# Some transfers move from SP to ACT's queue, and keys come in fewer, larger loads

## The chip, the cores and the metric

The kernel runs on one core of one Trainium2 chip. The metric is the time of one execution on the device in microseconds; the median of the runs shown is 1557.02 us. TensorE (PE), VectorE (DVE), ScalarE (ACT), GpSimd (POOL) and SyncE (SP) each work through an instruction list of their own in order. A transfer is issued by one engine's queue, and that engine goes on to its next instruction once the issue is done.

## The reference

One layer of an encoder runs on a prompt of 2048 tokens and a sample of 512, each of 1024 features, in float32:

```python
h = _rms_norm(x, norm_w)
proj = h @ w_in
# split in 15 parts: a_u, a_v, a_z, b_q, ..., c_q, c_k, c_v, c_z, d_x, d_z
y_a = _sgu_mixer(a_u, a_v, sgu_w, sgu_b) * silu(a_z)
y_b = _deltanet_mixer(b_q, b_k, b_v, ...) * silu(b_z)      # recurrence over chunks, both directions
y_c = _attention_mixer(c_q, c_k, c_v, ...) * silu(c_z)     # 4 heads of 64, 2 key heads, all tokens
y_d = _pool_mixer(d_x, pool_w, pool_scale) * silu(d_z)
return x + concat([y_a, y_b, y_c, y_d]) @ w_out
```

The attention's softmax runs over all tokens of a sequence: 2048 keys for each query of the prompt, 512 for the sample's.

## The kernel before

Tokens are taken in five blocks of 512, four of the prompt and one of the sample. Numbers that need more than half precision are split in two float16 parts whose products are summed, so most matrix products are three matmuls. Between stages the data pass through scratch tensors in DRAM.

`phase1` projects, convolves and normalises the delta-rule inputs. `phase2` runs in three passes over the blocks with other columns of `w_in`: rotary queries and keys (stored by `store_qk` to `QS` and `KS`), gates (`gz`, `zz`, `accz` on PE, from tiles `xs` that `load_xs` reads), pooling. Meanwhile `recurrence` steps through the chunks (tiles `kx`, `kv`, `at`, `tt` in; `up` on PE; `r`, `v`, `s` on ACT; `S` on DVE; `o` to `OD`). Each mixer's part of the concatenated row is written by `store_mix`: ACT writes `mixs`, DVE its second half, SP stores it to `MIX[b][f]`, f from 0 to 7.

`phase3` is attention and output projection. `load_kv` loads the keys of both key heads: `ka` holds both float16 parts of the keys on 128 rows, `kb` the first part again on 64 rows with a row of ones. `load_q` loads one head's queries of a block (`qa` twice the first part, `qb` the second). For a head, `row_max` computes scores `mp` on PE, DVE takes their maxima `mm`, and PE turns these (`mr`) for a row that ACT writes into `qb`. `attn` then goes through the keys in steps of 128: two matmuls give `sp`, ACT computes `e = exp(sp)` and its float16 copy `p`, DVE (every fourth time POOL) the second part of `p`, and PE adds twelve small matmuls to `O`. The next head's `row_max` is interleaved.

`outproj` loads a block's eight `MIX` parts (`mx`) and for each of four token tiles the input `xr`, computes `op` with 48 matmuls, adds on DVE to `y`, and stores `y`. Its matmuls are units that `pump` hands out one after each attention step at low priority, so that they fill PE.

The order on each engine isn't written by hand. A planner (`TileContext(..., schedule_with_timeline_sim=True)`) simulates the program with its own estimates of durations and takes, by priority, what is ready; each engine then runs its list in that order. Transfers of SP and ACT signal on eight completion semaphores that the planner gives out in turn over both queues, and each waits for the one before it on its semaphore.

Of the kernel before, what the change touches and what calls it, by code (L numbers as in the profile page):

```python
# [8 lines left out]
F16 = mybir.dt.float16  # L9
# [35 lines left out]
class Trunk:  # L45
# [94 lines left out]
    def consts(self, ctx):  # L140
        tc, nc, I = self.tc, self.nc, self.I
        self.cp = cp = self.pool(ctx, "const")
        self.nw = cp.tile([128, 8], F32, name="nw")
        self.ident = cp.tile([128, 128], F32, name="ident")
        self.ps = ctx.enter_context(tc.tile_pool(name="psum", bufs=1, space=PSUM))
        self.dram = ctx.enter_context(tc.tile_pool(name="dram", bufs=1, space=DRAM))
        NB, NT = self.NB, self.NT
        d = self.dram
        self.XS = [d.tile([128, 2, 8, 512], F16, name=f"xs{b}") for b in range(NB)]
        self.KX = [d.tile([4, 3, 64, 4, 2, 128], F16, name=f"kx{b}") for b in range(NB)]  # L150
        self.KV = [d.tile([4, 128, 512], F32, name=f"kv{b}") for b in range(NB)]
        self.MIX = [[d.tile([128, 2, 512], F16, name=f"mix{b}_{f}") for f in range(8)] for b in range(NB)]
        self.DG = [d.tile([128, 1024], F32, name=f"dg{b}") for b in range(NB)]
        self.XL = [d.tile([128, 1024], F32, name=f"xl{b}") for b in range(NB)]
        self.OD = [d.tile([128, 4, 256], F32, name=f"od{b}") for b in range(NB)]
        self.AT = [[d.tile([128, 2, 512], F16, name=f"at{t}_{i}") for i in range(2)] for t in range(NT)]
        self.SZ = [[d.tile([128, 512], F32, name=f"sz{b}_{f}") for f in range(4)] for b in range(NB)]
        self.QS = [d.tile([2, 4, 64, 512], F16, name=f"qs{b}") for b in range(NB)]
        self.KS = [d.tile([2, 2, 64, 512], F16, name=f"ks{b}") for b in range(NB)]
        self.TT = [[d.tile([128, 2, 512], F16, name=f"tt{t}_{i}") for i in range(2)] for t in range(NT)]  # L160
        self.DIF = [[d.tile([128, 512], F32, name=f"dif{b}_{f}") for f in range(2)] for b in range(NB)]
        self.MXD = [[d.tile([128, 512], F32, name=f"mxd{b}_{f}") for f in range(2)] for b in range(NB)]
        self.VT = [d.tile([128, 4, 260], F16, name=f"vt{b}") for b in range(NB)]
        self.LCJ = cp.tile([128, NT, 8], F32, name="lcj")
        self.C16 = cp.tile([128, NT, 3, 8], F16, name="c16")
        self.EG = [cp.tile([128, NT, 4], F32, name=f"eg{i}") for i in range(2)]
        self.NEG = [cp.tile([128, NT, 4], F32, name=f"neg{i}") for i in range(2)]
        self.KDS = [cp.tile([128, NT, 4], F32, name=f"kds{i}") for i in range(2)]
        self.EGT = cp.tile([128, NT, 8], F32, name="egt")
        self.RQK = cp.tile([128, NT, 8], F32, name="rqk")  # L170
# [393 lines left out]
    def phase2(self, names, ep, shared, stop=None):  # L564


        tc, nc, I = self.tc, self.nc, self.I
        V, A, G, PE = nc.vector, nc.scalar, nc.gpsimd, nc.tensor
        NB, W = self.NB, self.W2
# [111 lines left out]

        def store_qk(dst, s):

            if s.shape[2] == 2:
                for half in range(2):
                    for hl in range(2):
                        nc.sync.dma_start(dst[hl, :, half * 32:half * 32 + 32, :], s[:, hl, half, :])
            else:
                for half in range(2):
                    for hl in range(2):  # L690
                        nc.sync.dma_start(dst[hl, :, half * 32:half * 32 + 32, :], s[half * 64:half * 64 + 64, hl, 0, :])

        def rope_q(a, c, cs):

# [24 lines left out]
        def finish_k(b, kt, rt):  # L719
            s = ep.tile([128, 2, 2, 512], F16, tag="qk16", name="k16", bufs=1)[:, :, 0:1]  # L720
            with urgent():
                rb = norm_spread(rt, 2)
                V.tensor_tensor(kt, kt, rb, op=ALU.mult)
            A.activation(s[:, 0, 0], kt, AF.Copy)
            G.tensor_tensor(s[:, 1, 0], kt, s[:, 0, 0], op=ALU.subtract)
            store_qk(self.KS[b], s)

        def later(ins):

# [59 lines left out]
        for b in range(NB if stop is None else stop):  # L789
# [12 lines left out]
            if "QA" in names or "C" in names:  # L802
                t0 = b * 512 - (0 if b * 512 < self.NP else self.NP)
# [20 lines left out]
            if "C" in names:  # L824
                kt, ks = [ep.tile([128, 512], F32, tag=f"k{i}", name="k", bufs=1) for i in range(2)]
# [22 lines left out]
    def phase3(self, kp, ap, wp, ep, e5, rest, post):  # L848


        tc, nc, I = self.tc, self.nc, self.I
        V, A, G, PE, NB = nc.vector, nc.scalar, nc.gpsimd, nc.tensor, self.NB
        if True:
            wo = []
            for k in range(8):
                t = wp.tile([128, 2, 1024], F16, name=f"wo{k}")
# [9 lines left out]
            def load_q(b, h):  # L866
                qa = ap.tile([128, 512], F16, tag="qa", name="qa")
                qb = ap.tile([65, 512], F16, tag="qb", name="qb")
                for i in range(2):
                    nc.sync.dma_start(qa[i * 64:i * 64 + 64, :], self.QS[b][0, h])  # L870
                nc.sync.dma_start(qb[0:64, :], self.QS[b][1, h])
                return qa, qb

            def row_max(seq, b, h):
# [66 lines left out]
            def outproj(b):  # L941
                mix = []
                for f in range(8):
                    p, tag, n = (pool5(), "mx5", 7) if b % 2 and f < 7 else (ep, "mx4", 1) if b % 2 else (ep, "mx3", 8)
                    m = p.tile([128, 2, 512], F16, tag=tag, name="mx3", bufs=n)
                    nc.sync.dma_start(m, self.MIX[b][f])
                    mix.append(m)
                def units():
                    for tt in range(4):
                        t0 = b * 512 + tt * 128  # L950
                        xr = ep.tile([128, 1024], F32, tag="xr", name="xr")
                        nc.sync.dma_start(xr, I["x"][t0:t0 + 128, :])
                        y = ep.tile([128, 1024], F32, tag="y", name="y")
                        for n in range(2):
                            op = self.bank("X" + str(max(0, b - NB + 3)), [128, 512], "op")
                            for i, k in enumerate((0, 1, 6, 7, 2, 3, 4, 5)):
                                for j, (a, c) in enumerate(((0, 0), (0, 1), (1, 0))):
                                    PE.matmul(op, mix[k][:, a, tt * 128:tt * 128 + 128], wo[k][:, c, n * 512:n * 512 + 512],  # L958
                                              start=i + j == 0, stop=i == 7 and j == 2)
                                if i < 7:  # L960
                                    yield
                            V.scalar_tensor_tensor(y[:, n * 512:n * 512 + 512], op, IWS / MS, xr[:, n * 512:n * 512 + 512],  # L962
                                                   op0=ALU.mult, op1=ALU.add)
                            if n == 0:
                                yield
                        dst = self.O[0][t0:t0 + 128, :] if t0 < self.NP else self.O[1][t0 - self.NP:t0 - self.NP + 128, :]
                        nc.sync.dma_start(dst, y)
                        yield

                queue.append((clock[0] + LAG, units()))  # L970
# [3 lines left out]
            def pool5():  # L974
                if not p5:
                    p5.append(e5())
                return p5[0]
# [12 lines left out]
            def load_kv(s0, n):  # L990
                KA, KB = [], []
                vt = kp.tile([128, n // 512, 4, 2, 130], F16, tag=f"vt{s0}", name="vt3")
                for b in range(n // 512):
                    nc.sync.dma_start(vt[:, b].rearrange("p t k d -> p t (k d)"), self.VT[s0 // 512 + b])
                for kv in range(2):
                    ka = kp.tile([128, n], F16, tag=f"ka{s0}{kv}", name="ka")
                    kb = kp.tile([65, n], F16, tag=f"kb{s0}{kv}", name="kb")
                    (V if KBV else G).memset(kb[64:65, :], 1.0)
                    for b in range(n // 512):
                        kd = self.KS[s0 // 512 + b]  # L1000
                        c = slice(b * 512, b * 512 + 512)
                        for hl in range(2):
                            nc.sync.dma_start(ka[hl * 64:hl * 64 + 64, c], kd[hl, kv])
                        nc.sync.dma_start(kb[0:64, c], kd[0, kv])
                    KA.append(ka)
                    KB.append(kb)
                return s0, n, KA, KB, vt
# [481 lines left out]
```

## Time and profile before

| | |
|---|---|
| runs | 1556.85, 1557.02, 1558.1 us, median 1557.02 |
| profiled execution | 1564.48 us, its span 1562.7 us, mean clock granted to TensorE 0.965 |
| busy in the span | PE 91%, DVE 75%, ACT 51%, POOL 34% |
| transfers | 269.65 MB, nearly all issued by SP |

The profile shows one execution. A row of a wait reads: engine and line that waited, what ended the wait, then the sum in us, how often, and the longest. A row of the timeline has start, length, engine, line, operation, what it writes and reads with sizes, how many, and in brackets the idle time before. The letter q behind an engine's name is its sequencer, which waits and issues transfers; that time isn't in the engine's busy share. The profiled execution is 0.48% longer than the median of the runs, so differences are worked out within it and then put on the median.

### The profile page before, as it was taken

Reading aid. Unit: us, or ns where it says so; the run is one execution under the profiler, and the core shown is the slowest. Engines: PE = TensorE matmul, PEld = TensorE weight load, DVE = VectorE, ACT = ScalarE, POOL = GpSimd, SP = SyncE. Lnnn points to the kernel's source line nnn. Section 1 sums busy time; section 2 is a strip of 40 time slices with the busy share of each in tenths; the row PEclk is TensorE's granted clock in tenths of the full one; section 3 lists DMA queues with packets and bytes.
Section 4 is the critical chain, followed back from the end, with each engine's and each line's share of the span. In section 5 each row is a group of like instructions: output and inputs, shape, how many; then the busy total and the mean of one; then the engine's idle time right before and its main releaser. Section 6 shows DMA issues by size and latency. Waiting matters only on the chain. (4 is left out here: it accounts for less than half of the span.)

```text
span 1562.7 us, 34751 instructions
## 1 busy us (share of the span) xinstructions
PE 1418.7 (91%) x13420; PEld 782.8 (50%) x13420; DVE 1173.4 (75%) x2265; ACT 800.5 (51%) x1660; POOL 537.2 (34%) x646
## 2 busy tenths in 40 slices
PE   6999999988988887998988888889999999999998
PEld 3456555543444443454544444555555555555543
DVE  6338579966969888797987877899987787887611
ACT  5245434446555755465555224566766576576400
POOL 3220221034647744354353654663221121121100
PEclk9999999998998889899999999999999999999999
DMA  9845543465566786658678887643411411414333
GB/s 255 285 169 169 182 149 115 127 201 181 176 193 196 229 259 204 194 166 246 203 243 301 289 283 244 199 124 122 167 35 62 151 34 65 161 34 139 112 129 108
DMA packets 250830, 269.65 MB, mean 173 GB/s; under 512 B 95784, under 2 KB 176680, under 8 KB 250024
## 3 DMA queue, kind: packets, MB, share of 16 engines
q1 hardware_dynamic: 250264, 267.36, 54.4%
q8 instruction: 105, 1.72, 0.5%
q14 instruction: 61, 0.50, 0.1%
q0 software_dynamic: 400, 0.07, 0.1%
HBM read 175.66 MB, written 91.77 MB: 171 GB/s over the span
## 5 line engine op out<-in xcount | busy, mean ns | idle before, releaser
L127 PEld LDWEIGHTS <-w 128*128 128x128 f16 x2280 | 224.0, 101 | 303.2 <-issue 75.4
L127 PE MATMUL accz<-xs,w 128*128 128x512 f16 x960 | 239.4, 399 | 15.0 <-DMA xs<-xs 5.0
L958 PE MATMUL op<-wo,mx 128*128 128x512 f16 x960 | 226.4, 379 | 1.1 <-DVE y L962 0.7
L886 DVE TENSOR_REDUCE mm<-mp 128x1 f32<-128x512 f32 x272 | 179.1, 683 | 46.7 <-PE mp L884 46.2
L912 ACT ACTIVATE e<-sp 128x512 f32<-128x512 f32 x272 | 153.3, 596 | 75.6 <-PE sp L910 66.1
L916 POOL TENSOR_TENSOR p<-e,p 128x512 f16<-128x512 f32 x68 | 86.6, 1274 | 304.8 <-ACT p L915 286.5
L916 DVE TENSOR_TENSOR p<-e,p 128x512 f16<-128x512 f32 x204 | 167.4, 833 | 17.4 <-ACT p L915 17.3
L127 PE MATMUL acc<-xs,w 128*128 128x512 f16 x720 | 165.7, 388 | 2.7 <-ACT xs L288 1.5
L915 ACT ACTIVATE p<-e 128x512 f16<-128x512 f32 x272 | 160.9, 633 | 1.3
L921 PEld LDWEIGHTS <-p 128*128 128x128 f16 x3264 | 127.3, 97 | 59.2 <-DVE p L916 11.8
L921 PE MATMUL O<-vt,p 128*128 128x65 f16 (+1 forms) x3264 | 140.9, 193 | 7.1 <-DVE p L916 4.3
L958 PEld LDWEIGHTS <-mx 128*128 128x128 f16 x960 | 91.3, 98 | 104.8 <-issue 1.4
L884 PE MATMUL mp<-ka,qa 128*128 128x512 f16 x272 | 95.7, 382 | 12.1 <-DVE mm L886 5.3
L909 PE MATMUL sp<-qa,ka 128*128 128x512 f16 x272 | 103.5, 382 | 2.9 <-ACT e L912 2.7
L306 DVE SCALAR_TENSOR_TENSOR cv<-raw,convw,cv 128x512 f32<-128x512 f32 x120 | 88.0, 755 | 22.3 <-POOL raw L382 21.7
L910 PE MATMUL sp<-qb,kb 65*128 65x512 f16 x272 | 99.1, 382 | 1.3 <-ACT qb L894 1.3
L127 PE MATMUL accq<-xs,w 128*128 128x512 f16 x360 | 88.3, 389 | 10.7 <-DMA xs<-xs 8.6
L1271 POOL TENSOR_TENSOR kd<-kv,kds 128x512 f16<-128x512 f32 x40 | 45.0, 1126 | 126.1 <-PE up L1308 65.5
L400 PE MATMUL acct<-wtm,xs 128*128 128x400 f16 x480 | 83.8, 333 | 0.0
L291 POOL TENSOR_TENSOR xs<-xt,xs 128x512 f16<-128x512 f32 x36 | 49.2, 1389 | 76.2 <-ACT xs L288 75.9
L962 DVE SCALAR_TENSOR_TENSOR y<-op,xr 128x512 f32<-128x512 f32 x40 | 27.5, 687 | 58.8 <-PE op L958 58.7
L127 PE MATMUL accu<-xs,w 128*128 128x512 f16 x240 | 62.4, 409 | 4.7 <-DVE s L616 4.4
(316 smaller groups left out, 2506.2 us busy)
## 6 DMA issues: line engine op xcount, KB each, us to landing
xs<-xs SPq DMA_DIRECT2D x120, 256.0 KB
kx<-kx SPq DMA_DIRECT2D x80, 256.0 KB
at<-at SPq DMA_DIRECT2D x80, 256.0 KB
tt<-tt SPq DMA_DIRECT2D x80, 256.0 KB
xt<-in_xT SPq DMA_DIRECT2D x40, 256.0 KB
xs<-xs SPq DMA_DIRECT2D x5, 2048.0 KB
kv<-kv SPq DMA_DIRECT2D x40, 256.0 KB
mix<-mixs SPq DMA_DIRECT2D x40, 256.0 KB
```

Source lines behind the costliest of these rows:

```text
L127: mm = self.nc.tensor.matmul(ps, w[:, a, k, :], xk, start=k + i == 0, stop=k == 7 and i == 2)
L306: V.scalar_tensor_tensor(cv, raw[:, ct, i:i + 512], self.convw[:, ct, i:i + 1], cv, op0=ALU.mult, op1=ALU.add)
L400: PE.matmul(acc[:, 0:400], xs[:, a, k, tt * 128:(tt + 1) * 128], w[:, c, k, :], start=n == 0, stop=n == 23)
L884: PE.matmul(mp, qa[:, qt * 128:qt * 128 + 128], KA[h // 2][:, sc * 512:sc * 512 + 512], start=True, stop=True)
L886: V.tensor_reduce(mm[:, qt, sc:sc + 1], mp, axis=AX.X, op=ALU.max)
L909: PE.matmul(sp, KA[kv][:, c], qa, start=True, stop=False)
L910: PE.matmul(sp, KB[kv][:, c], qb, start=False, stop=True)
L912: A.activation(e, sp, AF.Exp)
L915: A.activation(p[:, 0], e, AF.Copy)
L916: (G if st % E8 == 1 else V).tensor_tensor(p[:, 1], e, p[:, 0], op=ALU.subtract)
L921: mm = PE.matmul(O[:, qt, 0:z - a], p[:, w, q], v[:, a:z], start=st == 0 and qt == 0 and i == 0, stop=st == nst - 1 and i == 2, skip_group ...
L958: PE.matmul(op, mix[k][:, a, tt * 128:tt * 128 + 128], wo[k][:, c, n * 512:n * 512 + 512], start=i + j == 0, stop=i == 7 and j == 2)
```

## The change

The loads of queries (`load_q`) and all four kinds of transfers of `outproj` (`mx`, `xr`, and `y` to both outputs) are issued by ACT instead of SP: 140 transfers. Keys lie in one scratch tensor for each sequence, by key head and float16 part, with all tokens of the sequence along a row, and `load_kv` loads each `ka` and `kb` at once: 8 loads instead of 30. The stores of keys stay 20, and keep rows of 512 tokens.

```diff
-        self.KS = [d.tile([2, 2, 64, 512], F16, name=f"ks{b}") for b in range(NB)]
+        self.KS = [d.tile([2, 2, 64, n], F16, name=f"ks{s0}") for s0, n in self.seqs]
...
-            store_qk(self.KS[b], s)
+            i = sum(b * 512 >= s0 + n for s0, n in self.seqs)
+            c = b * 512 - self.seqs[i][0]
+            for half in range(2):
+                for hl in range(2):
+                    nc.sync.dma_start(self.KS[i][:, hl, half * 32:half * 32 + 32, c:c + 512], s[half * 64:half * 64 + 64, hl, 0, :])
...
                 for i in range(2):
-                    nc.sync.dma_start(qa[i * 64:i * 64 + 64, :], self.QS[b][0, h])
-                nc.sync.dma_start(qb[0:64, :], self.QS[b][1, h])
+                    nc.scalar.dma_start(qa[i * 64:i * 64 + 64, :], self.QS[b][0, h])
+                nc.scalar.dma_start(qb[0:64, :], self.QS[b][1, h])
...
-                    nc.sync.dma_start(m, self.MIX[b][f])
+                    nc.scalar.dma_start(m, self.MIX[b][f])
...
-                        nc.sync.dma_start(xr, I["x"][t0:t0 + 128, :])
+                        nc.scalar.dma_start(xr, I["x"][t0:t0 + 128, :])
...
-                        nc.sync.dma_start(dst, y)
+                        nc.scalar.dma_start(dst, y)
...
-                    for b in range(n // 512):
-                        kd = self.KS[s0 // 512 + b]
-                        c = slice(b * 512, b * 512 + 512)
-                        for hl in range(2):
-                            nc.sync.dma_start(ka[hl * 64:hl * 64 + 64, c], kd[hl, kv])
-                        nc.sync.dma_start(kb[0:64, c], kd[0, kv])
+                    kd = self.KS[self.seqs.index((s0, n))][kv]
+                    nc.sync.dma_start(ka, kd.rearrange("i d t -> (i d) t"))
+                    nc.sync.dma_start(kb[0:64], kd[0])
```

The planner's order is the same on every engine up to the first loads of queries. Three places show how it moves after that. On SP, where the first keys are loaded among the recurrence's tiles, it stood before:

```order
L758 DMA ld<-dif_0_249 128x512
L994 DMA vt_13009<-vt_267 128x1040
L994 DMA vt_13009<-vt_268 128x1040
L1003 DMA ka<-ks_200 64x512
L1326 DMA od_133<-o 128x256
L1323 DMA ol<-od_131 128x256
L1267 DMA at_9289<-at_1_148 128x1024
L1262 DMA kx_9370<-kx_73 128x1024
L1265 DMA kv_9372<-kv_78 128x512
L1262 DMA kx_9455<-kx_71 128x1024
L1268 DMA tt_9375<-tt_0_233 128x1024
L1003 DMA ka<-ks_200 64x512
```

and now:

```order
L757 DMA ld<-dif_1_247 128x512
L999 DMA ka<-ks_200 128x2048
L1000 DMA kb<-ks_200 64x2048
L999 DMA ka<-ks_200 128x2048
L1263 DMA at_9201<-at_0_161 128x1024
L1399 DMA mix_1_89<-mixs 128x1024
L1263 DMA at_9286<-at_1_148 128x1024
L757 DMA ld<-dif_0_246 128x512
L1000 DMA kb<-ks_200 64x2048
```

All of the prompt's keys now stand within eight rows, ahead of loads that stood before the first of them.

On ACT, at the same time, the first two heads' queries come in. Before:

```order
L606 ACTIVATE gz<-accz 128x512 x2
L1304 ACTIVATE v_8983<-up 128x256
L1286 ACTIVATE s_9044<-S 128x256
L1401 ACTIVATE mixs<-gz 128x512 x2
L606 ACTIVATE zz<-accz 128x512
L1286 ACTIVATE s_9129<-S 128x256
```

and now:

```order
L606 ACTIVATE gz<-accz 128x512 x2
L1300 ACTIVATE v_8980<-up 128x256
L1282 ACTIVATE s_9041<-S 128x256
L1397 ACTIVATE mixs<-gz 128x512
L869 DMA qa<-qs_195 64x512 x2
L870 DMA qb<-qs_195 64x512
L869 DMA qa<-qs_195 64x512 x2
L870 DMA qb<-qs_195 64x512
L1282 ACTIVATE s_9126<-S 128x256
L1397 ACTIVATE mixs<-gz 128x512
L606 ACTIVATE zz<-accz 128x512
```

Six transfers now stand between the two writes of `mixs`.

On ACT in the attention, where a block's last mixes are written and the output projection loads the block before's and the next one's, it stood before:

```order
L1401 ACTIVATE mixs<-sz_18552 128x512
L912 ACTIVATE e<-sp 128x512 x3
L915 ACTIVATE p<-e 128x512
L1401 ACTIVATE mixs<-szb 128x512
L915 ACTIVATE p<-e 128x512 x2
L912 ACTIVATE e<-sp 128x512
L915 ACTIVATE p<-e 128x512
L912 ACTIVATE e<-sp 128x512
L1401 ACTIVATE mixs<-sz_18564 128x512
```

and now:

```order
L1397 ACTIVATE mixs<-sz_18527 128x512
L911 ACTIVATE e<-sp 128x512
L1397 ACTIVATE mixs<-szb 128x512
L911 ACTIVATE e<-sp 128x512 x2
L914 ACTIVATE p<-e 128x512
L945 DMA mx_20424<-mix_0_104 128x1024
L914 ACTIVATE p<-e 128x512
L945 DMA mx_20426<-mix_1_105 128x1024
L914 ACTIVATE p<-e 128x512
L945 DMA mx_20438<-mix_7_111 128x1024
L911 ACTIVATE e<-sp 128x512
L945 DMA mx_18605<-mix_2_98 128x1024
```

The loads of `mx`, on SP before, now stand between the exponentials; the last of them loads the mix that the second `mixs<-szb` row's activation began.

More of the change, by code (lines that the diff above doesn't have):

```diff
@@ L682, in store_qk @@
         def store_qk(dst, s):
-            if s.shape[2] == 2:
-                for half in range(2):
-                    for hl in range(2):
[L687 to L691, printed above, removed]
+            for half in range(2):
+                for hl in range(2):
+                    nc.sync.dma_start(dst[hl, :, half * 32:half * 32 + 32, :], s[:, hl, half, :])
         def rope_q(a, c, cs):
@@ L725, in finish_k @@
             G.tensor_tensor(s[:, 1, 0], kt, s[:, 0, 0], op=ALU.subtract)
-            store_qk(self.KS[b], s)
+            i = sum(b * 512 >= s0 + n for s0, n in self.seqs)
+            c = b * 512 - self.seqs[i][0]
+            for half in range(2):
+                for hl in range(2):
+                    nc.sync.dma_start(self.KS[i][:, hl, half * 32:half * 32 + 32, c:c + 512], s[half * 64:half * 64 + 64, hl, 0, :])
         def later(ins):
@@ L998, in load_kv @@
                     (V if KBV else G).memset(kb[64:65, :], 1.0)
-                    for b in range(n // 512):
-                        kd = self.KS[s0 // 512 + b]
-                        c = slice(b * 512, b * 512 + 512)
-                        for hl in range(2):
-                            nc.sync.dma_start(ka[hl * 64:hl * 64 + 64, c], kd[hl, kv])
-                        nc.sync.dma_start(kb[0:64, c], kd[0, kv])
+                    kd = self.KS[self.seqs.index((s0, n))][kv]
+                    nc.sync.dma_start(ka, kd.rearrange("i d t -> (i d) t"))
+                    nc.sync.dma_start(kb[0:64], kd[0])
                     KA.append(ka)
```

## The prediction

> **What bounds the kernel now.** First the page's share of engines and its 40 slices, then the same by stage, to see where TensorE idles at all.
>
> ```profile
> span 1562.7 us, 34751 instructions
> PE 1418.7 (91%) x13420; PEld 782.8 (50%) x13420; DVE 1173.4 (75%) x2265; ACT 800.5 (51%) x1660; POOL 537.2 (34%) x646
> PE   6999999988988887998988888889999999999998
> ...
> PEclk9999999998998889899999999999999999999999
> ```
>
> TensorE is busy for 91% of the span at an almost full clock; time can only come out of the other 9%, or be added to it. The two orders agree on every engine until the first loads of queries (SP issues them at 878 us before), so I cut what follows into stages there. The columns are the stretch, its length, then busy time of PE, its weight loads, DVE, ACT and POOL, the clock, the DMA engines' share and GB/s.
>
> ```profile
> 870.00:960.00 90.00, 79.75 (x754) 42.54 (x752) 65.50 (x121) 24.15 (x51) 44.04 (x47) 0.98 0.87 280
> 960.00:1020.00 60.00, 49.38 (x680) 30.80 (x679) 52.78 (x86) 32.48 (x68) 35.69 (x34) 0.97 0.64 200
> 1020.00:1100.00 80.00, 73.05 (x991) 44.50 (x988) 78.45 (x147) 50.42 (x99) 38.79 (x35) 1.00 0.40 125
> 1100.00:1410.00 310.00, 302.51 (x3231) 172.62 (x3230) 251.31 (x436) 205.41 (x384) 62.67 (x48) 1.00 0.26 86
> 1410.00:1500.00 90.00, 86.89 (x803) 48.20 (x802) 56.03 (x101) 44.57 (x84) 13.31 (x10) 0.98 0.39 127
> 1500.00:1563.00 63.00, 57.79 (x267) 25.85 (x265) 8.99 (x13) 0.00 (x0) 0.00 (x0) 1.00 0.35 121
> ```
>
> PE idles 10.3 us in 870 to 960, 10.6 in 960 to 1020 and 7.0 in 1020 to 1100: 27.9 us in all, while the delta-rule recurrence still runs and the DMA engines are busy up to 0.87. From 1100 to 1500, the attention proper, it idles 10.6 us in 400. So there is something to win in the first 230 us and next to nothing behind it, but in that second stretch ACT, which makes every exponential, can lose something: it is busy 205.41 of 310 us, 66%.
>
> **Fewer and earlier loads of keys (a gain).** These waits of PE name a DMA, the first two from 870 to 960, the third from 960 to 1020 (sum, times, longest):
>
> ```profile
> PE accz L127 <- DMA xs<-xs: 4.3, 5, 1.6
> PE mp L884 <- DMA ka<-ks: 2.0, 1, 2.0
> PE mp L884 <- DMA qa<-qs: 2.3, 1, 2.3
> ```
>
> What SP spends on these loads is in the rows of the lines (minimum, median, maximum ns of one issue, first and last start):
>
> ```profile
> L1003 SPq DMA_DIRECT2D ka<-ks x20: 444/592/1433, 902.9 to 951.5; - x20
> ...
> L1004 SPq DMA_DIRECT2D kb<-ks x10: 444/483/892, 909.2 to 952.1; - x10
> ...
> L870 SPq DMA_DIRECT2D qa<-qs x40: 444/496/1385, 877.9 to 1461.9; - x40
> ...
> L871 SPq DMA_DIRECT2D qb<-qs x20: 450/541/595, 879.7 to 1462.6; - x20
> ```
>
> Before, 20 x 0.592 + 10 x 0.483 = 16.7 us of SP's issue time go into keys between 903 and 952 us. Eight loads at the same medians are 4 x 0.592 + 4 x 0.483 = 4.3 us (their longer rows could cost up to the 1.433 that one took). That frees 12.4 us of SP, and the first two heads' six loads of queries another 4 x 0.496 + 2 x 0.541 = 3.1, in a stretch where SP issues nearly back to back:
>
> ```profile
> 908.70 0.47 SPq L1003 DMA_DIRECT2D ka<-ks  x1
> 909.22 0.59 SPq L1004 DMA_DIRECT2D kb<-ks  x1
> 909.86 1.23 SPq L1003 DMA_DIRECT2D ka<-ks  x2
> 911.18 0.53 SPq L1403 DMA_DIRECT2D mix<-mixs  x1
> ```
>
> The loads that PE waits for there (xs, 4.3 us) stand in this queue, and so do those of the recurrence. The order shows the prompt's four loads of keys close together, where 24 small ones were strewn over the recurrence's loads; so the first maxima and scores can start earlier, and PE gets other work to put into the recurrence's gaps. Between the bounds: at most the three waits above, 8.6 us, plus some of the other 19.3 us of idle time; at least nothing, since the DMA engines are busy 0.87 and the bytes of keys stay, in one burst of large transfers ahead of the recurrence's loads. I take 6 of the 8.6, because SP's issue time is measured and goes for certain, while what waits for ACT, DVE and POOL stays. The stores of keys are 20 as before with rows of 1 KB as before, a whole pass earlier: nothing.
>
> The first six loads of queries now stand on ACT between two writes of mixs. There ACT idled:
>
> ```profile
> 879.65 0.63 ACT L1401 ACTIVATE mixs<-gz 128x512 f16<-128x512 f32 x1 [4.70 <-DMA mix<-mixs]
> ...
> 884.05 0.42 ACT L1286 ACTIVATE s<-S 128x256 f16<-128x256 f32 x1 [3.29 <-DVE S L1310]
> ```
>
> 3.1 us of issues fit into 4.70 us of waiting for the buffer: cost nothing, and if a load has to wait for its completion semaphore (eight serve all of SP's and ACT's transfers in turn), the recurrence's next scaling, s at 884.05, has 3 us more of cover.
>
> **The issues on ACT (a loss).** The other moved lines cost SP this much apiece:
>
> ```profile
> L946 SPq DMA_DIRECT2D mx<-mix x40: 319/422/2362, 1089.1 to 1501.9; - x40
> ...
> L952 SPq DMA_DIRECT2D xr<-in_x x20: 377/425/840, 1091.3 to 1542.2; - x20
> ...
> L967 SPq DMA_DIRECT2D y_prompt<-y x16: 337/343/432, 1149.6 to 1525.1; - x16
> ```
>
> ACT issues no transfer before, so its price is SP's, an assumption. Behind the first two heads and ahead of the last exponential stand 18 heads' loads, 18 x (2 x 0.496 + 0.541) = 27.6 us, 35 of mx, 14.8, 14 of xr, 6.0, and 12 of y, 4.1: together 52.5 us on an engine that waits in 1020 to 1500 for PE this long:
>
> ```profile
> ACT qb L894 <- PE mr L892: 63.8, 13, 11.1
> ACT e L912 <- PE sp L910: 60.9, 51, 3.9
> ```
>
> 124.7 us of ACT's idle time end with PE, so on average there is room; a lump of 1.5 us ahead of an exponential is another matter. How much of ACT's extra work reaches PE? The nearest case is what ACT does beside e and p already, from 1100 to 1410 (count | busy, mean ns | idle before):
>
> ```profile
> L894 ACT ACTIVATE qb<-mr 1x512 f16<-1x512 f32 x11 | 6.5, 589 | 47.6 <-PE mr L892 47.5
> L1401 ACT ACTIVATE mixs<-szb 128x512 f16<-128x512 f32 x6 | 3.8, 634 | 1.0 <-DVE szb L1353 1.0
> L1335 ACT ACTIVATE osq<-ob 128x512 f32<-128x512 f32 x6 | 3.8, 632 | 0.2
> L1401 ACT ACTIVATE mixs<-sz 128x512 f16<-128x512 f32 x5 | 3.2, 631 | 3.1 <-DVE sz L938 3.1
> ```
>
> That is 17.3 us of extra work, and all of PE's idle time there, whatever its cause, is 7.5 us: a ratio of at most 0.43. The waits that name ACT, or DVE behind it, over the longer stretch 1020 to 1500 are
>
> ```profile
> PE O L921 <- DVE p L916: 4.0, 9, 1.0
> PE sp L909 <- ACT e L912: 1.9, 3, 1.3
> PE sp L910 <- ACT qb L894: 1.3, 3, 0.7
> ```
>
> so ACT alone accounts for 3.2 us in 480. Bounds for the 52.5 us: 0 (all in the waits for PE) to 0.43 x 52.5 = 23 us. I take 0.1, some 5 us: it is near what ACT's own waits say (3.2 us with extra work of that kind all along), and the planner has laid the new issues between exponentials and moved other rows for them.
>
> By the Trainium skill, "Perfetto Trace Analysis", section on the DVE and Act engine instruction, ACT's sequencer hands an activation to a wait queue and goes on to the next, while a transfer takes the sequencer itself; an issue would then run beside activations already handed over, and this term would be near 0 and the sum 1553 (an estimate). No row of before can show it, as ACT issues nothing there.
>
> **The waits that come with them (a loss).** A load of mx waits for the store of the same mix to land. From 1100 to 1500 SP waited for these, and for y:
>
> ```profile
> SPq L946 <- DMA mix<-mixs: 17.0, 9, 3.6
> SPq L967 <- DVE y L962: 170.4, 12, 25.0
> ```
>
> On ACT, e and p queue behind the same wait, and DVE, POOL and PE behind those. The 170.4 us are not lateness: SP had nothing else to do. On ACT the store of y stands behind exponentials whose scores PE computes about when it computes the last part of op, so I cost it at nothing beyond its issue; if DVE is late with y, p is late as well. The 17.0 us are real latency. In the order six activations and three issues, 6 x 0.6 + 3 x 0.42 = 4.9 us, now lie between mixs and the load of its mx, so most of each wait of 1.9 us on average is covered. Bounds 0 and 0.43 x 17.0 = 7.3 us; I take 2.
>
> **The end.** Behind the last attention ACT is idle (0 of 63 us), and PE has work until the last mixes land:
>
> ```profile
> 1500.11 2.22 SPq L946 DMA_DIRECT2D mx<-mix  x5
> ...
> 1506.09 51.97 PE L958 MATMUL op<-wo,mx 128*128 128x512 f16 x240 [0.27 <-DMA mx<-mix]
> ```
>
> A wait of 0.27 us is all that another queue could save. The last store of y goes out from ACT instead of SP: nothing.
>
> **Sum.** -6 + 5 + 2 = +1 us. The profiled execution took 1564.48 us, 1.8 more than its span and 7.5 more than the median of 1557.02; the difference is applied to the median: 1558 us, no change that can be measured (about 0.2%, 3.1 us, is what tells a change from none here).
>
> **Rivals.**
> - *The issues hide, the keys pay.* ACT's transfers fall into its 124.7 us of waiting for PE, and the three DMA waits of 8.6 us go whole: 1557 - 8.6 = 1548, or 1553 if my 6 us of gain is right and 2 us of waits stay. For it: the waits ended by PE are more than twice the 52.5 us. Against: half of them are single long waits ahead of qb, in which the next head's loads are long done.
> - *ACT becomes late in lumps.* Three loads of queries in a row hold exponentials for 1.5 us, ahead of qb as well, eighteen times; DVE's p and PE's O follow. At the ratio 0.43 this is 23 us, with -6 and +2 a time of 1576; at 0.25, 1566. It decides from a ratio of about 0.14 (7.2 us) on. For it: PE already waits for p nine times. Against: ACT at 66% plus 52.5 us in 480 stays below 80%.
> - *Nothing is freed.* The Trainium skill, "DMA: Bandwidth & Descriptors", section "Issuing engines are not separate DMA queues", says that a second issuing engine saves only issue time, as all share the 16 DMA engines. As a mechanism here: with these at 0.87 the burst of keys holds back xs and the recurrence's loads for as long as 22 issues did, the 6 us vanish, and it is 1557 + 7 = 1564. The rows of 870 to 960 bear the rule out in part: 0.87 leaves little room.
>
> **How the numbers follow.** Forecast (within 3.1 us of 1557): 0.35. Hidden issues: 0.31. Late in lumps: 0.20; nothing freed: 0.14. Faster 0.31, same 0.35, slower 0.34. The low end, 1547, is the whole 8.6 us of gain and a little of the recurrence's idle time; the high end, 1571, a ratio of about 0.3 with the gain halved; about one case in ten lies outside on either side. The forecast's own range is 1554 to 1560.
>
> **What would show it.** Keys: ka and kb in 8 issues before some 930 us, the waits for xs and ka gone, idle time of PE from 870 to 1100 near 22 us instead of 27.9. Issues: ACT's own queue shows 140 transfers of 0.3 to 0.6 us; idle time of PE from 1100 to 1500 near 17 us instead of 10.6, with ACT e, ACT p and DVE p as releasers. I am wrong if an issue on ACT takes 1 us or more, if PE waits for p by tens of us, or if the first stage keeps its idle time under other names.

## The result and the profile after

The changed kernel takes 1548.64 us (median of 11 runs, 1544.82 to 1555.45) against 1558.1 us for the kernel before (11 runs, 1553.47 to 1560.74): ratio 0.9941, 95% interval 0.9927 to 0.9956. It is faster by 0.6%, about 9 us; the forecast was no change. Two later comparisons, each with the kernel before on the same chip, gave 0.9932 (0.9910 to 0.9955) and 0.9935 (0.9912 to 0.9958).

The changed kernel's profiled execution has a span of 1546.8 us. Its stretches, with the same columns as before (length; busy time of PE, its weight loads, DVE, ACT, POOL; clock; DMA share; GB/s):

```profile
870.00:960.00 90.00, 80.01 (x808) 42.82 (x804) 69.24 (x123) 29.54 (x61) 43.63 (x46) 0.96 0.83 257
960.00:1020.00 60.00, 56.23 (x782) 34.81 (x779) 54.46 (x101) 33.95 (x72) 35.93 (x36) 1.00 0.62 203
1020.00:1100.00 80.00, 72.03 (x909) 44.03 (x908) 76.85 (x142) 47.07 (x94) 33.80 (x33) 0.98 0.43 139
1100.00:1410.00 310.00, 304.77 (x3238) 173.40 (x3235) 247.55 (x433) 207.70 (x389) 63.80 (x50) 1.00 0.25 86
1410.00:1500.00 90.00, 85.26 (x738) 45.79 (x737) 45.92 (x85) 35.25 (x65) 10.71 (x8) 1.00 0.42 144
```

TensorE idles 10.0, 3.8 and 8.0 us in the first three rows: 21.8 us where it was 27.9, and the forecast said 22. From 1100 to 1500 it idles 5.2 + 4.7 = 9.9 us, where the forecast said 17 and before showed 10.6.

The two spans differ by 15.9 us, more than the medians do. Part of that was there before the change could act, as one row shows: the scaling `s` that stood at 884.05 us before.

```profile
876.60 0.42 ACT L1282 ACTIVATE s<-S 128x256 f16<-128x256 f32 x1 [9.10 <-DVE S L1306]
```

It comes 7.5 us earlier, although both kernels run the same order up to there; the profiled execution of before, 1564.48 us, was itself 6.4 us above the median of its 11 runs. To leave this out, I cut both traces by events: from the start of the 281st of the recurrence's 576 matmuls `up<-s,kx` (the same one in every kernel here) to the end of the last of them, called the recurrence's end below, and from there to the end of the last O. Other matmuls of the recurrence go on behind this cut, the last starting at 1085.3 us before and 1082.9 after. First before, then after:

```profile
868.50:1073.70 205.20, 179.04 (x2149) 104.23 (x2146) 172.96 (x300) 90.03 (x184) 111.67 (x110) 0.98 0.67 212
1073.70:1484.20 410.50, 398.24 (x4241) 227.61 (x4240) 327.40 (x583) 266.12 (x498) 82.83 (x64) 1.00 0.30 98
```

```profile
861.10:1066.50 205.40, 186.80 (x2240) 108.70 (x2237) 176.76 (x311) 96.75 (x197) 112.58 (x113) 0.98 0.67 212
1066.50:1471.50 405.00, 391.89 (x4165) 223.33 (x4162) 317.64 (x571) 259.64 (x485) 81.30 (x63) 1.00 0.30 99
```

The recurrence's stretch has the same length, but TensorE idles 18.6 us in it instead of 26.2 and gets 91 more matmuls done. The attention's stretch is 5.5 us shorter with 76 fewer matmuls left in it, and its idle time, 13.1 us against 12.3, has hardly moved. What follows the last O takes 75.3 us instead of 78.5. Together 8.5 us: 7.6 of it idle time ahead of the recurrence's end.

What goes with it: the keys come in 8 issues, and the first O starts sooner (first and last start are the last two numbers; before, then after).

```profile
L921 PE MATMUL O<-vt,p x3264: 191/193/262, 962.7 to 1484.0; 128*128 128x65 f16 x128, 128*128 128x64 f16 x64
```

```profile
L920 PE MATMUL O<-vt,p x3264: 190/193/262, 942.7 to 1471.3; 128*128 128x65 f16 x128, 128*128 128x64 f16 x64
```

The loads of keys, and of queries and mixes, after (minimum, median, maximum ns of an issue; first and last start):

```profile
L999 SPq DMA_DIRECT2D ka<-ks x4: 320/360/577, 892.2 to 909.8; - x4
L1000 SPq DMA_DIRECT2D kb<-ks x4: 451/470/497, 893.0 to 910.4; - x4
```

```profile
L869 ACTq DMA_DIRECT2D qa<-qs x40: 452/463/1062, 866.9 to 1447.4; - x40
...
L945 ACTq DMA_DIRECT2D mx<-mix x40: 321/342/788, 1085.8 to 1489.0; - x40
```

The last load of keys goes out at 910.4 us instead of 952.1. Of the three waits for DMA, 8.6 us before, 2.0 are left (870 to 960; a wait of 0.7 us for a load of `kx` is new):

```profile
PE accz L127 <- DMA xs<-xs: 1.3, 2, 0.7
...
PE sp L908 <- DMA ka<-ks: 0.7, 1, 0.7
```

In the two further traces of the same kernel (under the experiments) these waits come to 2.5 and 5.2 us, at idle times of 18.4 and 18.0 us in the recurrence's stretch. So they aren't what decides it.

An issue on ACT costs no more than on SP (medians 0.463 us for `qa` and 0.342 for `mx` in these rows, 0.496 and 0.422 on SP before). ACT's waits from 1020 to 1500, where the new kinds appear:

```profile
ACT e L911 <- PE sp L909: 49.8, 36, 4.4
ACT qb L893 <- PE mr L891: 24.8, 6, 10.2
...
ACT p L914 <- issue: 6.9, 4, 2.6
...
ACT e L911 <- issue: 6.3, 2, 3.4
...
ACT p L914 <- DMA mix<-mixs: 3.6, 3, 2.3
```

ACT's 124.7 us of waiting for PE have shrunk to 74.6 in these two rows, and exponentials do wait behind issues. But TensorE seldom notices. Here is one such row of loads on ACT, and TensorE at the same time:

```profile
1255.82 1.55 ACTq L869 DMA_DIRECT2D qa<-qs  x2
1257.47 0.55 ACTq L870 DMA_DIRECT2D qb<-qs  x1
1258.06 0.60 ACT L911 ACTIVATE e<-sp 128x512 f32<-128x512 f32 x1 [3.37 <-issue]
```

```profile
1256.24 2.98 PE L957 MATMUL op<-wo,mx 128*128 128x512 f16 x13
```

```profile
1254.00:1262.00 8.00, 8.00 (x91) 4.50 (x88) 3.28 (x6) 3.71 (x8) 1.16 (x1) 1.00 0.27 92
```

The exponential is held for 3.37 us, and TensorE is busy all that time, from 1256.24 on with 13 matmuls of the output projection. Not all of the 3.37 us is issue time: the first load goes out 1.13 us into it, 0.20 us after the start of the old head's last score matmul `sp<-qb,kb` (1255.62), so ACT seems to wait there for a buffer of queries to come free, of which the kernel has two. The prediction has no term for that wait. In this trace there are 15 such rows of three query loads behind the recurrence; adding up TensorE's gaps from the first issue of each to 2.5 us after its last gives 1.6 us in all.

### The profile page after: what moved, and what is told of

Same layout as the page of the kernel before. It is cut to its first block, busy times and chain, and to the rows that moved or that the text cites. A ratio compares the mean times of both kernels' runs of the same rounds, so it can differ in the third digit from the quotient of the medians.

```text
span 1546.8 us, 34674 instructions
## 1 busy us (share of the span) xinstructions
PE 1412.3 (91%) x13420; PEld 780.3 (50%) x13420; DVE 1166.4 (75%) x2265; ACT 799.7 (52%) x1660; POOL 535.1 (35%) x646
## 5 line engine op out<-in xcount | busy, mean ns | idle before, releaser
L915 DVE TENSOR_TENSOR p<-e,p 128x512 f16<-128x512 f32 x204 | 160.3, 801 | 34.3 <-ACT p L914 31.9
L914 ACT ACTIVATE p<-e 128x512 f16<-128x512 f32 x272 | 162.1, 633 | 24.2 <-issue 6.9
L306 DVE SCALAR_TENSOR_TENSOR cv<-raw,convw,cv 128x512 f32<-128x512 f32 x120 | 87.7, 750 | 20.8 <-POOL raw L382 20.2
L1267 POOL TENSOR_TENSOR kd<-kv,kds 128x512 f16<-128x512 f32 x40 | 44.4, 1114 | 127.3 <-PE up L1304 81.5
L400 PEld LDWEIGHTS <-xs 128*128 128x128 f16 x480 | 46.9, 98 | 36.4 <-issue 3.3
```

Of the source, the lines that this page charges most:

```text
L306: V.scalar_tensor_tensor(cv, raw[:, ct, i:i + 512], self.convw[:, ct, i:i + 1], cv, op0=ALU.mult, op1=ALU.add)
L400: PE.matmul(acc[:, 0:400], xs[:, a, k, tt * 128:(tt + 1) * 128], w[:, c, k, :], start=n == 0, stop=n == 23)
L914: A.activation(p[:, 0], e, AF.Copy)
L915: (G if st % E8 == 1 else V).tensor_tensor(p[:, 1], e, p[:, 0], op=ALU.subtract)
```

## The experiments

Each kernel is timed against the kernel before on the same chip. "Idle" is TensorE's idle time in the two stretches above, the recurrence's and the attention's.

**The parts alone.** Keys alone (the loads of queries, `mx`, `xr` and `y` back on SP):

```diff
-  nc.scalar.dma_start(qa / qb / m / xr / dst, ...)
+  nc.sync.dma_start(qa / qb / m / xr / dst, ...)
```

> The keys' layout and their 8 loads alone; every transfer stays on SP. Theory A (the keys pay, ACT's transfers cost nothing): all of the gain of 9 us is here, ratio to the kernel before 0.994 +- 0.001, PE's idle time in 870 to 1100 us near 22 us. Theory B (the terms of the prediction, with the gain mis-sized: keys -16, ACT's issues and waits +7): ratio 0.990. Theory C (what pays is that SP is rid of 140 transfers, whichever engine takes them): about half here, 0.997.

Measured 0.9965 (0.9949 to 0.9980), -5.5 us. The queues alone (KS and its 30 loads as before, the five transfers on ACT):

> The loads of queries and the output projection's transfers on ACT, the keys as before (old layout, 30 loads). Theory A: ratio 0.999 to 1.001. Theory B: +7 us, 1.0045, with PE's idle time in 1100 to 1500 us near 17 us instead of 10.6. Theory C: 0.997, with the waits for xs in 870 to 960 us shorter than 4.3 us.

Measured 0.9979 (0.9963 to 0.9995), -3.3 us. The keys with the queries alone on ACT, and the keys with `mx`, `xr` and `y` alone on ACT:

> The keys' part, and only the loads of queries on ACT; mx, xr and y stay on SP. Theory A: as the whole change, 0.994. Theory B: keys -16, queries' 27.6 us of issues x 0.1 = +3: 0.992. Theory C: 0.9955, as the six early loads of queries are off SP.

> The keys' part, and only mx, xr and y on ACT; the loads of queries stay on SP. Theory A: 0.994. Theory B: keys -16, issues 24.9 us x 0.1 = +2.5 and the waits of mx +2: 0.9925. Theory C: 0.997, as all that leaves SP ahead of 1090 us is the keys' 22 issues.

Measured 0.9971 (0.9957 to 0.9985) and 0.9980 (0.9963 to 0.9998). Theory B is out: the queues cost nothing, they win. Theory A fails too: the keys alone give little more than half of the gain, and either half of the queues adds nothing to them. Theory C named the times of the first two and the last, but 0.9955 for the third. The two stretches of the keys alone:

```profile
862.70:1062.10 199.40, 182.72 (x2217) 106.61 (x2213) 169.90 (x308) 96.54 (x197) 113.10 (x111) 0.99 0.70 219
1062.10:1476.30 414.20, 395.95 (x4188) 225.55 (x4185) 328.83 (x574) 259.27 (x486) 83.24 (x64) 0.99 0.30 97
```

Ahead of the recurrence's end the keys alone win all there is (idle 16.7 us); in the attention they give back 6 (18.3 against 12.3). With a part of the transfers on ACT it is 20.1 and 22.4; with all of them 13.1 to 15.0. In the attention of the kernel with the queries alone on ACT, TensorE waits for loads, of queries above all:

```profile
PE mp L883 <- DMA qa<-qs: 7.8, 3, 2.9
```

These queries are issued by ACT, so they don't stand behind what SP's queue waits for. The longest of these waits has this ahead of it:

```profile
1083.41 1.35 SPq L945 DMA_DIRECT2D mx<-mix  x3
1084.85 0.85 SPq L951 DMA_DIRECT2D xr<-in_x  x2
1085.23 1.14 ACTq L869 DMA_DIRECT2D qa<-qs  x2
1092.82 0.59 PE L883 MATMUL mp<-ka,qa 128*128 128x512 f16 x2 [2.91 <-DMA qa<-qs]
```

SP puts out three `mx` of 256 KB and two `xr` of 512 KB just ahead of the queries and beside the first of them, the DMA engines are busy 0.98 of the time from 1085 to 1092, and TensorE gets the queries 6.5 us after their last issue. The whole change has these transfers in one list: there two `mx` and the queries (1086.85) go out first, the third `mx` (1088.96) and both `xr` behind them, and no wait for queries shows in its attention. The other two waits also follow two `mx` that SP issues 1 to 2 us ahead. So one queue may win because it keeps the attention's loads in the order of their use; that is read from these places, and no run tests it alone.

**The whole again, and which transfer matters.** The whole change twice more, and the whole with `y`, with `xr` and `y`, or with `mx` left on SP:

> The whole change again, beside the other three on one chip. Theory D (the parts work together: keys win about 9 us of TensorE's idle time up to the end of the recurrence, and lose 6 behind it unless the loads of queries and the output projection's transfers leave SP together): 0.994 again, clearly below the two halves' 0.997 and 0.998. Theory E (the parts simply add, the rest is scatter between chips and orders): 0.9945 too, as 0.9965 x 0.9979 = 0.9944. If the first result was scatter: 0.997.

> The whole change once more, on the same chip as the kernel beside it: 0.993 to 0.995 as in its two comparisons so far.

```diff
-  nc.scalar.dma_start(dst, y)
+  nc.sync.dma_start(dst, y)
```

> The whole change, but the 16 stores of y stay on SP, where their waits for DVE (up to 25 us each) hold back the stores of mix behind them. Theory D: the attention loses part of what it kept, idle time of TensorE behind the recurrence 17 to 20 us instead of 13, ratio 0.997. Theory E: y is 16 of 140 transfers, 0.9945. Prediction's terms: 4.1 us of issues off ACT x 0.1, 0.994.

```diff
-  nc.scalar.dma_start(xr, I["x"][t0:t0 + 128, :])
+  nc.sync.dma_start(xr, I["x"][t0:t0 + 128, :])
   (and y as above)
```

> The whole change, but xr and y stay on SP, so that ACT issues the loads of queries and mx alone. If ACT's issues cost 0.1 of their time: 10.1 us less of issues, 0.993. If it matters that the attention's transfers stand in one queue: 0.996 to 0.997, as when mx, xr and y all stayed on SP. If ACT's issues are hidden and y and xr are indifferent: 0.993 to 0.994.

```diff
-  nc.scalar.dma_start(m, self.MIX[b][f])
+  nc.sync.dma_start(m, self.MIX[b][f])
```

> The whole change, but the 40 loads of mx, which wait for the store of their mix to land, stay on SP. If these waits on ACT cost what the prediction took (+2) and their 14.8 us of issues 0.1: 3.5 us less, 0.9915. If what made the keys and the queries alone worse (0.9971) is that the loads of mx stand in SP's queue with their waits: 0.997, with idle time of TensorE behind the recurrence of 18 us or more. If neither: 0.993 to 0.994.

Measured: whole 0.9932 and 0.9935, so the keys' and the queues' parts add (theory E's 0.9944 lies in all three intervals), while the two halves of the queues do not; `y` on SP 0.9929 (0.9911 to 0.9947); `xr` and `y` on SP 0.9949 (0.9930 to 0.9967); `mx` on SP 0.9976 (0.9957 to 0.9995). So the stores of `y`, with all their waits, are indifferent (theory D named the wrong transfer), `xr` nearly so, and without the loads of `mx` on ACT most of the queues' gain is gone (the intervals lie edge to edge: 0.9957 at its lower end, 0.9955 to 0.9958 at the upper ends of the whole change). With `mx` back on SP, SP and TensorE show in the attention:

```profile
SPq L945 <- DMA mix<-mixs: 24.2, 11, 5.7
```

```profile
PE op L957 <- DMA mx<-mix: 4.0, 2, 3.4
```

SP waits 24.2 us for mixes to land, and with it whatever stands behind; `mx` itself comes up to 3.4 us late. On ACT the same wait holds p for 3.6 us in all. That SP's waits are what delays the rest is read from these rows, not separately shown. Nor do the loads of `mx` win by themselves: with `mx`, `xr` and `y` on ACT and the queries on SP the kernel measured 0.9980, no better than the keys alone.

**SP's issues ahead of the recurrence's end.** The whole change with 30 loads of keys out of the new layout; with 22 small loads that nothing reads behind the 8; with the first two heads' queries on SP; and with keys and values on ACT:

```diff
-  nc.sync.dma_start(ka, kd.rearrange("i d t -> (i d) t"))
-  nc.sync.dma_start(kb[0:64], kd[0])
+  for c in range(0, n, 512):
+      for hl in range(2):
+          nc.sync.dma_start(ka[hl * 64:hl * 64 + 64, c:c + 512], kd[hl, :, c:c + 512])
+      nc.sync.dma_start(kb[0:64, c:c + 512], kd[0, :, c:c + 512])
```

> The whole change, but the keys come from the new layout in 30 loads of 512 tokens, as before. If the 22 issues taken from SP are what pays (the prediction's reason for its -6): the keys' part is lost, 0.998, as the queues alone. If the layout or the place of the loads in the order pays: 0.994 to 0.995, as the whole change.

```diff
+  dm = kp.tile([64, 11, 16], F16, ...)
+  for j in range(11):
+      nc.sync.dma_start(dm[:, j], kd[0, :, j * 16:j * 16 + 16])
```

> The whole change, with 22 more loads on SP, 11 right behind each sequence's loads of keys: 64 rows of 32 bytes each, into a tile that nothing reads. So SP issues as many transfers there as before the change, but the keys are still there early. If SP's issue time is what paid (the prediction's reason): the keys' part is lost, 0.998 to 1.000, like the 30 loads. If it is that the keys land earlier and the attention's matmuls can fill the recurrence's gaps: 0.993 to 0.995, first O still near 940 us.

```diff
+  dma = nc.sync if b == 0 and h < 2 else nc.scalar
-  nc.scalar.dma_start(qa / qb, ...)
+  dma.dma_start(qa / qb, ...)
```

> The whole change, but the first two heads' six loads of queries go back to SP, at about 870 us, ahead of the keys: 3.1 us of SP's issue time. At 0.7 us for each issue (the 22 small loads): +4, 0.9965, and a wait for xs above 3 us. By the prediction (nothing but their share of the freed time): +1, 0.9945.

```diff
-  nc.sync.dma_start(ka / kb[0:64] / vt[:, b], ...)
+  nc.scalar.dma_start(ka / kb[0:64] / vt[:, b], ...)
```

> The whole change, and the keys' 8 loads and the 5 loads of values beside them on ACT too: 13 issues or some 5.4 us less on SP between 870 and 960 us, on an ACT that is busy there 30 of 90 us. If SP's issue time in this stretch is on the path at the price that the 22 small loads had (15 us, 0.7 each): -9, ratio 0.988. If only what waits for the keys themselves mattered: 0.993 to 0.995. If ACT's issues cost there what they cost when the queries were split (0.5 to 0.75 of their time): +3, 0.996.

Measured 0.9998 (0.9979 to 1.0017), 1.0036 (1.0020 to 1.0051), 1.0023 (1.0002 to 1.0044) and 1.0101 (1.0070 to 1.0131). The 30 loads lose the whole gain in spite of the new layout, so it isn't the layout that pays but the number of loads, or the order that the planner makes with it (2122 matmuls ahead of the recurrence's end, as with the queues alone):

```profile
857.20:1060.10 202.90, 178.76 (x2122) 103.71 (x2119) 171.41 (x295) 88.55 (x182) 112.03 (x112) 0.97 0.68 216
```

Idle 24.1 us again, and 118 matmuls fewer than in the whole change. The other three are not a price per issue: 22 small loads cost 15 us, six loads of queries 14, and taking 13 issues off SP, expected to win 9 us, lost 25. They moved the planner's order, all in one direction. With keys and values on ACT the first O starts at 916 us, and the two stretches read

```profile
863.10:1075.50 212.40, 195.58 (x2440) 117.14 (x2437) 186.47 (x329) 106.70 (x219) 121.54 (x116) 0.98 0.66 212
1075.50:1496.60 421.10, 394.36 (x3961) 217.93 (x3960) 312.41 (x554) 247.91 (x463) 78.18 (x61) 0.97 0.29 94
```

200 matmuls more than in the whole change were put ahead of the recurrence's end; the stretch got 6 to 10 us longer, and in the attention behind it TensorE idles 26.7 us, twice as long. So an earlier attention alone doesn't win here (ACT also has 13 issues more), and these three don't tell SP's issue time from the order.

**ACT's issues.** Each load of queries in four of 16 rows, in two of 32; then, from the second block on, only `qb` in four column parts, all on ACT or the three added ones on SP, and in two:

```diff
+  for j in range(0, 64, 16):    (or 32)
       for i in range(2):
-          nc.scalar.dma_start(qa[i * 64:i * 64 + 64, :], self.QS[b][0, h])
+          nc.scalar.dma_start(qa[i * 64 + j:i * 64 + j + 16, :], self.QS[b][0, h][j:j + 16])
       (qb alike)
```

> The whole change, with each load of queries cut into four of 16 rows: 240 transfers on ACT instead of 60, the same bytes. At some 0.45 us that is 180 x 0.45 = 81 us more of issue time on ACT, 73 of them behind the first two heads. If ACT's issues are hidden in its waits for TensorE: within 3 us of the whole change (0.994 to 0.996). At the prediction's 0.1 of them: +7, 0.9985. At its upper bound 0.43: +31, 1.014.

> The whole change, each load of queries in two of 32 rows: six issues in a row ahead of each head, some 2.7 us instead of 1.4, 60 issues or 27 us more on ACT. The split by 4 added 81 us of issues and cost 36 us. If the price is proportional (0.45): +12, 1.001. If short rows of issues hide and only long ones hold exponentials: +0 to +4, 0.994 to 0.996.

```diff
-  nc.scalar.dma_start(qb[0:64, :], self.QS[b][1, h])
+  w = 128 if b else 512         (256 for two parts)
+  for c in range(0, 512, w):    (nc.sync where c > 0, in the second kernel)
+      nc.scalar.dma_start(qb[0:64, c:c + w], self.QS[b][1, h][:, c:c + w])
```

> The whole change, but from the second block on qb comes in 4 loads of 128 columns, all on ACT: 48 issues more, 21.6 us, all in the attention and none in the recurrence's stretch, whose order stays. If ACT's issues are hidden there: 0.993 to 0.995. If they cost 0.45 to 0.75 of their time, as the split queries suggest: +10 to +16, 1.000 to 1.004. The prediction's 0.1: +2, 0.995.

> The same 4 loads, but the 3 added ones on SP: the same transfers without ACT's time. If it is ACT's issue time that costs: 0.993 to 0.995 here, clearly below the kernel with all four on ACT. If it is that the queries come in smaller pieces and later: as that one.

> The whole change, but from the second block on qb comes in 2 loads of 256 columns on ACT: 16 issues more, some 7.2 us, four in a row ahead of a head instead of three. Three more (48 issues) cost 20 to 22 us against the whole change, three more on SP 10. If ACT's issues cost in proportion: a third, +7, 0.998 to 1.000. If rows of three or four hide and only longer ones hold exponentials: 0.993 to 0.995.

Measured 1.0169 (1.0148 to 1.0189), 1.0068 (1.0045 to 1.0090), 1.0081 (1.0054 to 1.0107), 1.0004 (0.9978 to 1.0029) and 0.9966 (0.9950 to 0.9982). The first two also changed the order ahead of the recurrence's end (2143 and 2425 matmuls there against 2240). The first three came out above every value expected for them (1.014, 1.001 and 1.004), and so did the fourth, which was to be 0.993 to 0.995 if ACT's time were all that costs. The last three leave the place where the attention's scores start in TensorE's order as it was. One chip gave 12 us (0.77 points) between the same 48 transfers on ACT and on SP, with intervals apart: ACT's time does cost. Against the whole change, one issue more per head costs 0.31 points, 4.8 us (intervals overlapping a little), three more about 22 us. Around the rows of query loads TensorE's gaps add up to 1.6 and 2.0 us in two traces of the whole change (rows of three), 6.8 with four in a row and 13.0 with six; with three on ACT and three beside them on SP it is 5.1. With six in a row, ACT's e and p wait 32.4 and 22.5 us behind loads of `qb`. The gaps explain only half of the 22 us. The attention's stretch, first of the whole change, then with the added loads on SP, then with all on ACT:

```profile
1068.40:1476.20 407.80, 393.56 (x4163) 223.90 (x4160) 317.48 (x572) 259.85 (x485) 81.17 (x63) 1.00 0.30 98
```

```profile
1060.10:1475.30 415.20, 399.14 (x4163) 226.01 (x4160) 317.87 (x571) 259.26 (x485) 82.39 (x63) 0.98 0.30 97
```

```profile
1062.80:1495.30 432.50, 408.85 (x4225) 230.15 (x4224) 320.92 (x578) 261.88 (x492) 86.06 (x64) 0.97 0.29 94
```

The first two have the same 4163 matmuls, and TensorE is busy 5.6 us longer in the second, at a granted clock of 0.98 instead of 1.00; the third stands at 0.97. How a wait becomes a lower clock is told at the end.

All kernels in one table (idle and matmuls from rows like those above; "half" is the time in both stretches that TensorE's clock stood at one half):

| kernel | ratio | idle, recurrence | its matmuls | idle, attention | half |
|---|---|---|---|---|---|
| before | 1 | 26.2 | 2149 | 12.3 | 10.2 |
| whole (three traces) | 0.9941, 0.9932, 0.9935 | 18.6, 18.4, 18.0 | 2240, 2239, 2243 | 13.1, 15.0, 14.2 | 10.2, 10.2, 17.1 |
| keys alone | 0.9965 | 16.7 | 2217 | 18.3 | 10.2 |
| queues alone | 0.9979 | 22.4 | 2122 | 14.5 | 17.1 |
| keys, queries on ACT | 0.9971 | 17.2 | 2240 | 20.1 | 17.1 |
| keys, mx, xr, y on ACT | 0.9980 | 17.7 | 2221 | 22.4 | 10.2 |
| whole, y on SP | 0.9929 | 16.7 | 2241 | 13.6 | 13.7 |
| whole, xr and y on SP | 0.9949 | 16.6 | 2240 | 15.2 | 17.1 |
| whole, mx on SP | 0.9976 | 18.6 | 2239 | 18.6 | 10.2 |
| 30 loads of keys | 0.9998 | 24.1 | 2122 | 13.6 | 10.2 |
| 22 small loads | 1.0036 | 24.1 | 2287 | 20.3 | 23.9 |
| first six on SP | 1.0023 | 20.2 | 2346 | 19.1 | 23.9 |
| keys, values on ACT | 1.0101 | 16.8 | 2440 | 26.7 | 34.1 |
| queries split by 2 | 1.0068 | 18.6 | 2425 | 23.6 | 37.5 |
| queries split by 4 | 1.0169 | 22.0 | 2143 | 36.3 | 44.4 |
| qb in 2 on ACT | 0.9966 | 18.1 | 2217 | 14.3 | 17.1 |
| qb in 4 on SP | 1.0004 | 19.9 | 2241 | 16.1 | 17.1 |
| qb in 4 on ACT | 1.0081 | 18.4 | 2174 | 23.7 | 30.7 |

Each row of idle times is one execution, so a difference of 1 or 2 us there says nothing. No kernel beat the whole change beyond its interval.

## Why the prediction was wrong

- **Keys, -6: the size right, the reason only in part.** Alone they measured -5.5 us, and in the whole change the idle time from 870 to 1100 came out at 21.8 us against the 22 named. But the 6 us were taken from the waits for DMA, because SP's issue time goes, and the largest of these, for `xs`, 4.3 us before, stays with the keys alone (it is 1.3 to 3.2 in the three traces of the whole change):

```profile
PE accz L127 <- DMA xs<-xs: 4.3, 2, 2.5
```

TensorE still idles 9.5 us less ahead of the recurrence's end (16.7 against 26.2) and gets 68 more matmuls done there, which fits the other reason that the prediction names: the attention starts sooner (12.5 us in the whole change, 20.0 in the rows less the 7.5 that were there before) and fills gaps of the recurrence. That 6.0 us come back as idle time in the attention and bring -9.5 near the -6 is luck.

- **The first six loads on ACT, 0: nearly right.** `s` waits for DVE there, not for the loads. But the second write of `mixs`, 4.40 us ahead of `s` before, now comes 0.33 behind it, with `zz` and `gz` behind that, and TensorE waits for both (before, then after, 870 to 960):

```profile
PE accu L127 <- DVE zz L607: 0.3, 1, 0.3
```

```profile
PE accu L127 <- DVE zz L607: 1.1, 1, 1.1
PE up L1287 <- ACT gz L606: 1.0, 1, 1.0
```

That is 1.8 us in place of nothing. The wait for `zz` is 1.1 us in the other two traces of the whole change too, and 0.3 with the keys alone and with the first six loads on SP.

- **ACT's issues, +5: too high.** TensorE's gaps around the query loads, 27.6 of the 52.5 us priced, are 1.6 to 2.0 us, near the 2.8 that 0.1 gives. For `xr` and `y`, 10.1 us, taking them off ACT won nothing (0.9949 and 0.9929 against 0.9932 to 0.9941); for the 14.8 of `mx` no run tells the price from the gain. The ratio 0.1 was no constant: the cover is the output projection's matmuls laid beside a row of loads. A fourth issue in the row costs 4.8 us, a fourth to sixth 22, of which some 10 come with the same loads on SP as well.
- **The price of the queues, +5 and +2: the step that failed.** Both terms count only what the transfers and their waits do on ACT. That they leave SP was put at nothing beyond the issue time of the first six, and the sum so had a loss of 7 us. The runs show a gain: -3.3 us with the queues alone, and -3.7 to -5.1 on top of the keys. Nearest to its cause stands `mx`, whose 17.0 us of waits on SP the prediction priced only on ACT: with `mx` back on SP the kernel loses 0.35 to 0.44 points, 5.5 to 7 us, and TensorE waits for `mx` and `qa`. But `mx` without the queries won nothing, so this is no term that could be added by itself, and whether SP's waits or the order in which two queues mix their loads does it stays open. For `y`, the sentence that SP has nothing else to do held.
- **The sum.** The two parts alone, -5.5 for the keys and -3.3 for the queues, make -8.8, near the -9 to -11 that the whole change measured in its three comparisons; the forecast was +1. The prediction named the right stretch and size for the first, and a loss that isn't there for the second.
- **The rivals.** "The issues hide, the keys pay" gave 1548, the time measured, by luck: its first half nearly holds, but it lacks the gain from leaving SP, and the keys give 5.5 alone rather than 8.6. "Late in lumps" is what the split queries do, from four issues in a row on. "Nothing is freed" fell as a time, 1564, since the keys alone win 5.5 us; but their wait for `xs` stays, as it said.
- **What a sequencer holds.** Issues begin while ACT still computes:

```profile
1223.72 0.63 ACT L914 ACTIVATE p<-e 128x512 f16<-128x512 f32 x1
1223.86 0.45 ACTq L869 DMA_DIRECT2D qa<-qs  x1
1224.25 0.58 ACT L911 ACTIVATE e<-sp 128x512 f32<-128x512 f32 x1
1224.65 0.46 ACTq L869 DMA_DIRECT2D qa<-qs  x1
1225.21 0.55 ACTq L870 DMA_DIRECT2D qb<-qs  x1
1225.81 0.63 ACT L914 ACTIVATE p<-e 128x512 f16<-128x512 f32 x1 [0.97 <-ACT e L911]
```

The first load goes out 0.14 us into p, the second 0.40 us into e, so 1.5 us of issues cost ACT 0.97. The Trainium skill, "Perfetto Trace Analysis", section on the DVE and Act engine instruction, has the sequencer put an activation into a wait queue and go on, which agrees with these rows; by it the term would have been near 0 and the sum 1553, closer than mine. The activation behind a row of issues is held all the same, in the row shown further up until 0.04 us after the last of them.

## What to carry to other kernels

When transfers are moved to a second queue, price what they stop holding back on the old queue, and which loads they no longer run ahead of, as well as what they hold on the new one; and move together those that feed the same stage, since here either half of them won nothing. Issues on an engine that feeds TensorE are free only as far as other matmuls are laid beside them, so look for the filler behind each row of issues and keep the rows short. And where a planner writes the order, a small edit far from the critical wait can cost more than the edit is worth: time every part, and compare the matmuls done by a common event.

## What the runs showed of the hardware

I had not expected that a short wait costs twice. TensorE's clock drops to one half in steps of 3.4 us. The kernel with `qb` in four loads on ACT, two windows that follow each other:

```profile
1354.19:1357.59 3.40, 1.46 (x17) 0.60 (x14) 2.68 (x10) 0.17 (x1) 0.82 (x1) 1.00 0.94 296
1357.62:1361.01 3.39, 2.99 (x8) 1.04 (x8) 1.90 (x6) 1.55 (x3) 0.00 (x0) 0.50 0.06 12
```

TensorE idles 1.94 us of the first, and the second runs at 0.50. Over the attention of 20 traces, cut by the clock's own steps into 2362 windows of 3.41 us, the next window was at half clock after all 15 with 2 us of idle time or more, after 34 of 41 with 1.6 or more, and after 12 of the 2240 with less than 1. A window at half clock costs about 1.7 us more, half of its length. From the recurrence's 281st update on, time less idle time less half of the low-clock time is 639.5 to 645.7 us in all 20 traces, while the time itself goes from 684.9 to 724.3: idle time and the low clock make up most of the difference between these kernels. The kernel before and two of the three traces of the whole change have the same 10.2 us at half clock in the two stretches, so for the change itself the clock decides nothing; but half of that, 5 us, stood in what the prediction took for busy time that can't be won. The Trainium skill, "TensorE: Matmul & The Clock Gate", section "Part 1: The HAM clock gate", gives windows of about 3.4 us and half rate after an idle one; the steps agree, but here a window half idle was enough.

What stays open: why `mx` and the queries win only together, whether SP's issue time or the order pays for the keys, what the order alone costs where the small loads and the first six queries moved it, and why the same 48 loads cost 10 us on SP.
